# A hybrid pooling / matrix-memory layer on one core: single first transfers, unread products, w_up's sums loaded in mid-step, and the last group's second norm moved into the feed-forward half

## The chip, the core and the metric

The kernel runs on one core of a Trainium2 chip. A core has a matrix engine (TensorE, PE in the profile; PEld are its weight loads), three engines for elementwise work (VectorE = DVE, ScalarE = ACT, GpSimd = POOL), and a queue engine (SyncE = SP) that does little but issue DMA transfers; ACT can issue transfers too. Each engine works through its own list of instructions in order and waits for the others on semaphores. On-chip memory is SBUF; products of PE land in eight PSUM banks.

The metric is the device time of one execution in microseconds (us). Matrix products have fp32 data, most of them split into two parts (`fp32r`, high and low) with three passes per product; a product of two plain fp32 operands shows as two records in the trace.

## The reference

One layer over 2112 tokens (2048 of a prompt and 64 of a sample with its own states), model width 1024, then a final norm. Cut to what matters:

```
mod = silu(c) @ w_ada + b_ada                 # shift, scale, gate: two times three vectors of 1024
h   = rmsnorm(x, g1) * (1 + sc1) + sh1
proj = h @ w_in                               # 512 pooling columns, q, k, v, o of 4 heads x 128, gates
pool_out = causal moving means of widths 2, 4, 8, 16, then a 128 x 128 product per group
hs  = mLSTM(q, k, v, gates)                   # chunked matrix memory, per-head norm, times sigmoid(o)
x   = x + gt1 * (concat(pool_out, hs) @ w_out)
h2  = rmsnorm(x, g2) * (1 + sc2) + sh2
up  = h2 @ w_up                               # 1024 -> 2 x 2816
conv = causal depthwise convolution of width 3 over tokens
x   = x + gt2 * ((silu(g) * a) @ w_down)      # 2816 -> 1024
y   = rmsnorm(x, g_final)
```

Also returned are the pooling, memory and convolution states at the end.

## The kernel before

Activations are held transposed, features on the 128 partitions and tokens along the free axis, so a row of 1024 features is eight tiles (`KD = 8`).

**Attention half.** Four groups of tokens: three of 512 and a last one of 576 (512 of the prompt and the 64 of the sample). Per group: the first norm, the projections, the memory and the pooling mixer, the output projection `outproj` with the residual, whose result goes to DRAM as `x2d`. A scheduler orders the instructions of this half by priorities and costs of its own, so an edit in one place can move instructions elsewhere; only the first part of group 0, `first()`, is in the order as written (`tc.manual_schedule`).

`first()` begins with no data on the chip. The first 512 tokens of x come as eight tiles `x0[k]`, then V (a table with small vectors, and the 128 x 128 identity), then the four loads of the first quarter of the modulation weights (`w_mod`). ACT squares each x0 tile (L984), DVE adds the squares into two sums (L989), `rstd_cols` (L485) adds over partitions with one-column products (L489) and makes the reciprocal root (DVE L491, then POOL). `mod_q` (L918) makes a quarter of the modulation vectors: 32 products of a two-column operand (L923), a copy by ACT (L930), a transpose on PE (L932). Four products (L1001) spread the norm's factors over partitions into the bank `pr`; DVE multiplies x by it (L1005); ACT shifts and scales (L953), and the first projection (L1028) can start. Products whose result nobody reads stand in between (L991 on each x0 tile, and L1010).

**Background work.** Lists `bg[0]` to `bg[4]` hold generators; `tick(i)` advances one of them by one step between pieces of the main work. In groups 1 to 3 these run: `ada` (the remaining modulation vectors from `w_ada`: loads `raw<-w_ada` and multiply-adds on DVE, L197), `fold`, and `up_sums` (L819). The latter works ahead for the feed-forward half: for each of 44 pieces of w_up it loads four parts (`w<-w_up`, two transfers, L824), takes sums and differences in four DVE operations (L838, L839, L841, L842) and stores the piece (`wsum<-w`, L847). The order of these instructions among themselves is kept; where they stand among others is the scheduler's choice. There are four buffers for the pieces. `gemm` (L435) is the product loop, with line L445 for its products. In the middle of each group `lstm` copies gate values out of PSUM: CL (after which a cumulative product L1201 follows), GL (which products at L1255 free their bank by), then kw (read by the products L1280).

**Last group's second norm.** `outproj` ends with the squares of the new x for the second norm: an ACT square (L476, L479) and a DVE add (L480) per row, in `sq_acc`. For the last group the sum then goes to `stat2` (L578), which waits twelve ticks in the feed-forward half and calls `rstd_cols`.

**Feed-forward half.** All in the order as written. Three groups of 704 tokens, in four parts of the 22 blocks of 128 inner features. Seven products per block instead of eight come from sums and differences of inputs and weights (`norm_sums` L771 makes those of the inputs, hx: DVE L745 and others, ACT L738; `wsum` has those of the weights). `product` (L525, products L1531) works with weights that ACT and DVE split into two parts (L379, L382); ACT evacuates (s at L1570, u at L1579 and L1594), the convolution and gate follow, and the down projection is L1807 with its residual on DVE (L1823).

**The end.** The last part of the last group is done in two sections of tokens, 448 and 256 (`ENDS`). For each, `final_end` adds the squares over partitions (L1705), makes the factors (DVE L1661, POOL L1663), spreads them by products (`spread`, L1721), multiplies (DVE L1746, POOL L1759) and stores y. `m2_ps` and `mm_ps` hand out PSUM banks in rotation.

## Time and profile before

| | us |
|---|---|
| median of 3 runs (2225.89 to 2227.29) | 2227.15 |
| the profiled execution | 2230.81 |
| its span from first to last instruction | 2229.0 |
| PE busy | 2208.9 |
| DVE busy | 1572.2 |
| ACT busy | 1000.4 |
| POOL busy | 192.5 |
| moved by DMA | 487.26 MB, 219 GB/s in the mean |

All times below that are called "at" are us from the start of the span. A row of a timeline gives start, duration (of the merged instructions), engine, line, operation, output <- inputs by the program's names, shapes and count; in brackets stands how long the engine had been idle and what ended that. The clock of PE is given in the windows as a share of its full speed. A row of the chain of waits has start, duration and what it was.

### The profile page before, as it was taken

How to read it: one execution, taken by the hardware profiler on the slowest of the kernel's cores; microseconds unless marked ns; L12 is line 12 of the kernel's file. 1: busy time of each engine (PE TensorE's matmuls, PEld its weight loads, DVE VectorE, ACT ScalarE, POOL GpSimd, SP SyncE). 2: the span in 40 equal slices, each digit the busy share in tenths (PEclk: the TensorE clock that was granted, in tenths of full speed). 3: DMA queues.
4: the chain of work that ended last, by engine and by line, in shares of the span. 5: the costliest groups of instructions: out<-in, count | busy, mean ns of one | idle time of the engine just before them, and what ended most of it. 6: DMA issues, size and time to landing. Idle time of an engine off the chain costs nothing.

```text
span 2229.0 us, 37990 instructions
## 1 busy us (share of the span) xinstructions
PE 2208.9 (99%) x13744; PEld 2102.7 (94%) x13744; DVE 1572.2 (71%) x2888; ACT 1000.4 (45%) x1981; POOL 192.5 (9%) x474
## 2 busy tenths in 40 slices
PE   8999999999999999999999999999999999999998
PEld 7888888888899999999999999999999999999998
DVE  5867668757955688687858587777766675757475
ACT  4644335234333455454536354545444343445254
POOL 0010000001000100010000210100001210101012
PEclk9999999999999999999999999999999999999999
DMA  9977997988879485747557775466458655353442
GB/s 350 330 251 228 300 305 254 306 286 266 296 253 299 148 269 164 243 163 270 179 176 243 263 263 176 156 213 198 143 160 290 196 167 167 111 171 116 145 148 81
DMA packets 284708, 487.26 MB, mean 219 GB/s; under 512 B 24640, under 2 KB 88512, under 8 KB 284520
## 3 DMA queue, kind: packets, MB, share of 16 engines
q1 hardware_dynamic: 275080, 462.52, 63.2%
q10 hardware_dynamic: 9440, 22.32, 2.6%
q8 instruction: 108, 1.77, 0.3%
q14 instruction: 80, 0.66, 0.1%
HBM read 378.68 MB, written 106.06 MB: 217 GB/s over the span
## 4 chain that ended last, share of the span: by engine, by line
PE 94%; DMA 3%; DVE 2%; issue 1%; SPq 0%; ACT 0%; POOL 0%; POOLq 0%; DVEq 0%; ACTq 0%
PE mm L1531 40%; PE mm L1807 23%; PE mm L445 23%; PE mm L1091 1%; DMA raw<-w_ada 1%; PE m L1280 1%; PE m L1300 1%; PE m L1302 1%; PE m L1265 1%; DMA wsum<-w 1%; PE mm L1028 1%; PE p L1028 1%; PE m L923 0%; PE m L1255 0%; DVE scr L237 0%
## 5 line engine op out<-in xcount | busy, mean ns | idle before, releaser
L1531 PE MATMUL mm<-hx,wt 128*128 128x352 f32 x5544 | 897.9, 323 | 1.9 <-ACT s L1570 1.3
L1531 PEld LDWEIGHTS mm<-hx,wt 128*128 128x128 f32 x5544 | 892.8, 188 | 2.6 <-ACT s L1570 1.6
L1807 PE MATMUL mm<-av,wt 128*128 128x352 f32 (+2 forms) x3168 | 514.5, 323 | 0.0
L1807 PEld LDWEIGHTS mm<-av,wt 128*128 128x128 f32 x3168 | 509.6, 188 | 1.2
L445 PE MATMUL mm<-hl,wt 128*128 128x512 f32 (+2 forms) x1920 | 389.7, 358 | 0.0
L379 ACT ACTIVATE wt<-raw 128x512 fp32r<-128x512 f32 (+3 forms) x518 | 286.2, 574 | 215.6 <-PE mm L445 77.6
L382 DVE TENSOR_TENSOR wt<-raw,wt 128x512 fp32r<-128x512 f32 (+3 forms) x518 | 324.4, 641 | 78.4 <-ACT wt L379 75.6
L445 PEld LDWEIGHTS mm<-hl,wt 128*128 128x128 f32 x1920 | 315.4, 189 | 52.5 <-issue 5.3
L1823 DVE SCALAR_TENSOR_TENSOR x<-mm,MOD,x 128x352 f32<-128x352 f32 (+4 forms) x224 | 106.5, 526 | 133.1 <-PE mm L1807 132.9
L445 PE MATMUL mm<-mx,wt 128*128 128x512 f32 (+1 forms) x960 | 185.3, 354 | 0.0
L445 PEld LDWEIGHTS mm<-mx,wt 128*128 128x128 f32 x960 | 159.1, 188 | 25.4
L1518 DVE SCALAR_TENSOR_TENSOR tg<-eg,V,tg 128x704 f32<-128x704 f32 (+1 forms) x132 | 125.7, 953 | 53.9 <-ACT tg L1513 51.6
L382 DVE TENSOR_TENSOR wt<-wt 128x512 fp32r<-128x512 f32 x176 | 121.7, 692 | 36.9 <-ACT wt L379 36.9
L1518 DVE SCALAR_TENSOR_TENSOR ta<-ea,V,ta 128x704 f32<-128x704 f32 (+1 forms) x132 | 125.7, 952 | 5.2 <-ACT ta L1513 2.6
L379 ACT ACTIVATE wt<-wt 128x512 fp32r<-128x512 f32 x176 | 108.3, 622 | 18.3 <-DMA wt<-wsum 14.6
L1579 ACT ACTIVATE u<-mm 128x352 f32<-128x352 f32 x66 | 30.7, 465 | 169.5 <-PE mm L1531 162.0
L1539 DVE TENSOR_TENSOR eg<-mm,u 128x352 f32<-128x352 f32 x154 | 70.2, 468 | 41.2 <-ACT u L1594 27.1
L1639 DVE TENSOR_TENSOR av<-tg,av 128x704 fp32r<-128x704 f32 (+1 forms) x88 | 60.6, 709 | 53.8 <-ACT av L1634 53.8
L1625 ACT ACTIVATE tg<-tg 128x704 f32<-128x704 f32 (+1 forms) x66 | 52.4, 794 | 78.5 <-DVE tg L1518 78.5
L1570 ACT ACTIVATE s<-mm 128x352 f32<-128x352 f32 x66 | 30.7, 465 | 111.4 <-PE mm L1531 106.9
L1091 PE MATMUL mm<-wt,hl 128*128 128x256 f32 (+1 forms) x576 | 70.7, 282 | 0.0
L1091 PEld LDWEIGHTS mm<-wt,hl 128*128 128x128 f32 x576 | 69.8, 188 | 0.9 <-issue 0.6
(293 smaller groups left out, 1954.3 us busy)
## 6 DMA issues: line engine op xcount, KB each, us to landing
raw<-w_up SPq DMA_DIRECT2D x198, 256.0 KB, 4.0
wt<-hl_kept SPq DMA_DIRECT2D x96, 512.0 KB, 6.0
wt<-wsum SPq DMA_DIRECT2D x176, 256.0 KB, 4.0
wt<-wsplit SPq DMA_DIRECT2D x88, 512.0 KB, 4.6
raw<-w_down SPq DMA_DIRECT2D x96, 256.0 KB, 3.0
w<-w_up SPq DMA_DIRECT2D x88, 256.0 KB, 4.0
wsum<-w SPq DMA_DIRECT2D x44, 512.0 KB, 5.1
wsplit<-wt SPq DMA_DIRECT2D x44, 512.0 KB, 3.3
```

What stands on the lines that cost most here:

```text
L379: act.activation(u.w[:, 0, :u.n], u.raw[:, :u.n], AF.Copy)
L382: dve.tensor_tensor(out=u.w[:, 1, :u.n], in0=u.raw[:, :u.n], in1=u.w[:, 0, :u.n].bitcast(F32), op=ALU.subtract)
L445: pe.matmul(ps[bi][:, :hi - lo], U[:, a, k % 4 * P:(k % 4 + 1) * P], mv[k][:, b, lo:hi], start=(at == 0 and pi == 0), stop=(k == order[-1] ...
L1028: pe.matmul(to[ti][:, :n], h[k][:, b, ti * P:(ti + 1) * P], w[:, a, k % 2 * n:(k % 2 + 1) * n], start=(hv == 1 and k == 0 and (a, b) == (0 ...
L1091: pe.matmul(ps[ti][:n, :cols], h[4 * kh + k4][:, b, lo:lo + n], U[:, a, k4 % 2 * cols:(k4 % 2 + 1) * cols], start=(kh == 0 and k4 == 0 and ...
L1518: dve.scalar_tensor_tensor(out=t[:, :E], in0=ext[:, j:j + E], scalar=wc(j, f), in1=t[:, :E], op0=ALU.mult, op1=ALU.add)
L1531: pe.matmul(ps[:, :FH], U[:, a, kc * P:(kc + 1) * P], Bo.at(nm, kc, b), start=(first and kc == 0 and pi == 0), stop=(kc == 3 and pi == 2), ...
L1539: dve.tensor_tensor(out=ext[:, d:d + b - a], in0=ps[:, a:b], in1=u[:, a:b], op=ALU.add)
L1625: act.activation(self.tg[:, :E], self.tg[:, :E], AF.Silu)
L1639: dve.tensor_tensor(out=self.d[:, 1, a:b], in0=self.tg[:, a + 2 * s:b + 2 * s], in1=self.d[:, 0, a:b].bitcast(F32), op=ALU.subtract)
L1807: pe.matmul(ps[i][:, :hi - lo], U[:, a, k % 4 * P:(k % 4 + 1) * P], av[k][:, b, lo:hi], start=(k == 0 and (a, b) == PASSES[0]), stop=(k == ...
L1823: dve.scalar_tensor_tensor(out=x3[n][:, a:b], in0=ps[i][:, a - lo:b - lo], scalar=gt2(n, s), in1=x3[n][:, a:b], op0=ALU.mult, op1=ALU.add)
```

## The change

- The eight tiles of x0 come in eight transfers of 256 KB, four each from SP and ACT, instead of four of 512 KB.
- In `first()`, squares 6 and 7 are not added by DVE; four sums go to PE, which adds them over partitions by accumulating one-column products into a bank that is cleared beforehand. The factors are spread by one product of `ones` with a diagonal matrix that DVE makes, instead of four products with the identity. Eight products that nobody reads stand between the eight steps of `mod_q(0)`, and the two at L1010 write to another bank.
- Two small operations on V (into M and GH) move from the front of DVE's list to behind `first()`.
- In `up_sums` a step i with 0 < i < len - 2 loads piece i + 2 ahead of its four DVE operations, where before it loaded piece i + 3 after them, ahead of the store.
- For the last group the squares and adds leave `outproj`. `stat2` reloads the eight rows from `x2d` and does squares, adds and `rstd_cols` in steps in the feed-forward half.
- In the last section of the end, the bank for the sums over partitions is taken and cleared before the last row's products, and products that nobody reads are put in two places (`busy`).

```diff
-    for k in range(0, KD, 2):
-        (act if k % 4 else nc.sync).dma_start(out=pair_of(x0[k:k + 2]), in_=xT[k:k + 2, :, 0:GT].rearrange("k p t -> p k t"))
+    for k in range(KD):
+        (act if k % 2 else nc.sync).dma_start(out=x0[k], in_=xT[k, :, 0:GT])
...
-    def stat2(o, ssum):
-        out = RS2[:, 4 * o.g:4 * o.g + len(o.chunks)]
-        for _ in range(12):
-            yield
-        rstd_cols([ssum], o, out)
+    def stat2(o):
+
+        def load(k):
+            x = fscr()
+            nc.sync.dma_start(out=x[:, :o.T], in_=x2d[k, :, o.t0:o.t0 + o.T])
+            return x
+        nx = [load(0), load(1)]
+        ssum = fscr("ssum")
+        yield
+        for k in range(KD):
+            x = nx.pop(0)
+            yield
+            act.activation((x if k else ssum)[:, :o.T], x[:, :o.T], AF.Square)
+            yield
+            if k:
+                dve.tensor_tensor(out=ssum[:, :o.T], in0=ssum[:, :o.T], in1=x[:, :o.T], op=ALU.add)
+            if k + 2 < KD:
+                nx.append(load(k + 2))
+        yield
+        rstd_cols([ssum], o, RS2[:, 4 * o.g:4 * o.g + len(o.chunks)])
         yield
...
-                if o.last:
-                    ssum = fscr("ssum")
             for n, x in zip(rows, xs):
-                sq_acc(ssum, x[:, :o.T], o.T, n == 0)
+                if not o.last:
+                    sq_acc(ssum, x[:, :o.T], o.T, n == 0)
         if o.last:
-            bg[0].append(stat2(o, ssum))
+            bg[0].append(stat2(o))
...
                 yield
                 yield
+                if 0 < i < len(todo) - 2:
+                    nx.append(load(*todo[i + 2]))
...
                 yield
-
-                if i + 3 < len(todo):
-                    nx.append(load(*todo[i + 3]))
                 pin(nc.sync.dma_start(out=wsum[f, :, :, c:c + 256], in_=w))
...
+            cols = third.tile([P, 512], F32, tag="bank", name="cols")
+            dve.memset(cols[:, :4], 0.0)
             for k in range(KD):
                 x, sq = x0[k], scr()
                 act.activation(sq[:, :GT], x, AF.Square)
-                if k < 2:
+
+                if k < 2 or k > 5:
                     sums.append(sq)
...
             silu()
+            for sq in sums:
+                for ti in range(4):
+                    pe.matmul(cols[:, ti:ti + 1], sq[:, ti * P:(ti + 1) * P], ones[:, 0:1], start=False, stop=sq is sums[-1],
+                              skip_group_check=True)
             rs = sm.tile([P, 5], F32, tag="rs", name="rs")
-            rstd_cols(sums, o0, rs)
+            dve.tensor_scalar(out=rs[:, :4], in0=cols[:, :4], scalar1=1.0 / D, scalar2=EPS, op0=ALU.mult, op1=ALU.add)
+            pool.tensor_tensor(out=rs[:, :4], in0=rs[:, :4], in1=half[:, :4], op=ALU.pow)
             mod = mod_q(0)
-            for _ in range(KD + 1):
+            for k in range(KD):
                 next(mod)
 
+                pe.matmul(ptq[:, 256:384], x0[7][:, :P], x0[7][:, :P], start=True, stop=True)
+            next(mod)
+            dg = scr()
+            dve.tensor_tensor(out=dg[:, :GT].rearrange("p (t c) -> p t c", c=P),
+                              in0=ident.unsqueeze(1).broadcast_to([P, 4, P]),
+                              in1=rs[:, 0:4].unsqueeze(2).broadcast_to([P, 4, P]), op=ALU.mult)
             pr = third.tile([P, 512], F32, tag="bank", name="pr")
-            for ti in range(4):
-                pe.matmul(pr[:, ti * P:(ti + 1) * P], rs[:, ti:ti + 1].broadcast_to([P, P]), ident, start=True, stop=True)
+            pe.matmul(pr, ones, dg[:, :GT], start=True, stop=True)
...
             for _ in range(2):
-                pe.matmul(psq[:, :256], x0[7][:, :P], x0[7][:, :256], start=True, stop=True)
+                pe.matmul(ptq[:, 256:], x0[7][:, :P], x0[7][:, :256], start=True, stop=True)
...
                     ps_v = first()
+                    dve.tensor_copy(M[:, GT + 1:GT + 2], RV[:, 2:3])
+                    dve.tensor_scalar(out=GH, in0=V[:, V_GH:V_GH + NH], scalar1=0.5, scalar2=None, op0=ALU.mult)
...
-    late, YLATE = [], 6
+    late, early, YLATE = [], [], 6
+
+    def busy(n):
+
+        for _ in range(n):
+            pe.matmul(early[1][:, :P], ident, ident, start=True, stop=True)
...
-        ps = m2_ps()
+        ps = m2_ps() if lo == 0 else early[0]
...
-        if lo > 0:
-            dve.memset(ps[:, :len(tiles)], 0.0)
...
         if lo > 0:
             late[0](YLATE)
+            busy(3)
         stat_cols(ps, rs, [n for (t, n) in tiles])
...
                 if ends and n == KD - 1:
+                    if lo > 0:
+                        busy(2)
                     sq7 = fscr()
...
+                    if ends and n == KD - 1 and secs[0][0]:
+
+                        early.extend([m2_ps(), mm_ps()])
+                        dve.memset(early[0][:, :2], 0.0)
                     down(ps, rows[n], range(nf), secs, ends)
```

2 lines of the change are left out of this document (removed).

## The prediction

> **What bounds the kernel now.** I read the page first, then the list of PE's waits, then the windows around those waits. The first rows below are the page's busy times and the shares of its chain of waits; then the list of PE's waits (us in total, times, longest).
>
> ```profile
> PE 2208.9 (99%) x13744; PEld 2102.7 (94%) x13744; DVE 1572.2 (71%) x2888; ACT 1000.4 (45%) x1981; POOL 192.5 (9%) x474
> PE 94%; DMA 3%; DVE 2%; issue 1%; SPq 0%; ACT 0%; POOL 0%; POOLq 0%; DVEq 0%; ACTq 0%
> ```
>
> ```profile
> PE m L991 <- DMA mx<-xT: 5.7, 1, 5.7
> PE m L1255 <- DVE GL L237: 2.0, 1, 2.0
> PE m L1280 <- DVE kw L237: 2.0, 1, 2.0
> PE mm L1531 <- ACT s L1570: 1.3, 1, 1.3
> PE m L489 <- DVE scr L989: 1.0, 2, 0.9
> PE m L1721 <- POOL rs L1663: 1.0, 1, 1.0
> PE m L1705 <- DVE m L1702: 0.9, 1, 0.9
> PE mm L1028 <- ACT hl L953: 0.6, 1, 0.6
> PE mm L1531 <- DVE hx L745: 0.6, 1, 0.6
> ```
>
> TensorE (PE) is busy 99% and is 94% of the chain. So no edit to another engine counts unless it ends one of these nine waits (15.1 us together), or shortens a stretch in which PE is busy with less than products. Three places hold nearly all: the start (5.7 + 1.0 + 0.6), the middle of each attention group (2.0 + 2.0) and the seam to the feed-forward half with the end (1.3 + 0.6 + 1.0 + 0.9). Beside that PE loses time to its granted clock; the windows are cut where it changes (columns: busy time of each engine, clock, DMA share, GB/s).
>
> ```profile
> 10.64:14.06 3.42, 2.38 (x16) 1.84 (x14) 2.53 (x5) 1.50 (x4) 0.00 (x0) 1.00 1.05 387
> 14.06:17.47 3.41, 3.41 (x47) 2.80 (x50) 0.16 (x1) 0.00 (x0) 1.10 (x2) 0.50 1.05 390
> 17.47:20.88 3.41, 3.41 (x40) 2.65 (x33) 0.00 (x0) 0.81 (x2) 0.00 (x0) 0.50 1.06 387
> 20.88:24.29 3.41, 2.79 (x16) 2.02 (x16) 2.98 (x9) 2.25 (x5) 0.00 (x0) 1.00 1.05 396
> 263.23:266.64 3.41, 1.45 (x10) 1.00 (x9) 2.51 (x5) 0.19 (x1) 0.00 (x0) 1.00 0.80 267
> 266.64:270.06 3.42, 3.42 (x13) 3.00 (x13) 3.03 (x9) 0.00 (x0) 0.00 (x0) 0.50 1.04 335
> 2219.05:2222.46 3.41, 1.51 (x12) 1.29 (x11) 2.94 (x8) 1.02 (x3) 0.81 (x2) 1.00 0.68 259
> ```
>
> The clock halves for a whole window of 3.41 us after a window that was poor in work: 1.45 of 3.41 busy, 1.51 busy (what comes after it is in the last rows of this text, 1.79 against 1.19 us for eight like records), but also 2.38 busy, mainly with one-column products. The window from 14.06 was fully busy with one- and two-column products and did not bring it back; the next, half of it 128-column products (L1001), did. So thin products hardly count, by this trace.
> The Trainium skill (TensorE: Matmul & The Clock Gate, "What's actually happening") says that the gate watches a free-running window of 3413 ns and halves the clock after an idle window; the length agrees with the 3.41 us here, the condition does not, since none of these windows was idle.
>
> The sum goes against the profiled execution, 2230.81 us (span 2229.0). That is 3.7 us over the median of the runs, 2227.15; I subtract the sum from the median.
>
> **A, the start** (single transfers; no wait for V; sums 6 and 7 added by PE; L1001 as one product; unread products between).
>
> ```profile
> 5.67 6.16 PE L991 MATMUL m<-mx 128*128 128x256 f32 x16 [5.67 <-DMA mx<-xT]
> 15.58 3.59 PE L923 MATMUL m<-mx,CA 128*2 128x128 f32 x64
> 19.10 1.99 PE L1001 MATMUL pr<-V,rs 128*128 128x128 f32 x8
> 20.93 0.27 PE L932 MATMUL m<-V,scr 128*128 128x128 f32 x1
> 21.04 1.03 PE L1010 MATMUL m<-mx 128*128 128x256 f32 x4
> 22.69 2.04 PE L1028 MATMUL mm<-wt,hl 128*128 128x264 f32 x11 [0.62 <-ACT hl L953]
> 33.00 1.86 PE m L923 x64
> 9.35 0.14 DVE L1420 COPY M<-V 4x1 f32<-4x1 f32 x1 [7.95 <-DMA V<-vecs]
> 820.14 0.99 PE m L489 x10
> ```
>
> Before, the products on x begin at 5.67 with the landing of a 512 KB pair, and take 6.16 us without a gap. DVE's adds wait 7.95 us behind a copy from V, so the sums on PE end only where L923 begins, at 15.58. After: half the pair is 256 KB, and with two queues in flight 0.5 MB less stands before the first landing; at the 390 GB/s of the windows that is 1.3 us, so PE starts at about 4.4 and is through at 10.5. The Trainium skill (DMA: Bandwidth & Descriptors, "Bandwidth") speaks against this edit: transfers below 1 MiB get less of the peak, 341 GB/s at 1 MB and 138 at 64 KB; an estimate of 250 GB/s at 256 KB by it would land the 2 MB of x about 3 us later. The window from 20.88, where 264 KB and 256 KB loads stand in the queue, moved 396 GB/s, so I add nothing for it.
>
> The copies from V leave the queue ahead of the adds, four adds remain instead of six, and V's later issue (its queue slot now waits for a landing) holds up only SiLU and the ident product, both needed after 12 us. On PE there are now 32 one-column passes instead of 16. At full clock one costs 0.99/10 = 0.10 us, so 3.2 us: 10.5 to 13.7, against 15.58 before. Then come 64 records of the modulation, 1.86 us at full clock (the row at 33.00) or 3.59 at half, and between them 16 records of unread 128-column products, 0.15 each at full (1.19/8, the row at 2213.61 below) or 0.22 at half (1.79/8): 4.3 us at full, 7.1 at half. One 512-column product replaces L1001: as many columns as the four L1010 records, 1.0 us at full clock against 1.99. From the small transpose (L932) to the first projection (L1028) it stays 22.69 - 20.93 = 1.76 us.
> At full clock throughout: 13.7 + 4.3 + 1.0 + 1.8 = 20.8. If x's products run partly at full clock (they begin earlier, so an earlier window may already count) all of it comes some 0.7 sooner: 20.1. If the clock is half from 13.7 until 17.5, when a window with the unread products has passed, 3.8 of the 7.1 us are done, the rest takes 2.0, and it is 22.3; with a window more at half clock about 23.2. Gain: 2.6 at best, -0.5 at worst. I take 1.9, the value at full clock, because the window from 17.47 shows that such a mixture raises it. The loads are no obstacle: the DMA share is full in these windows with the same bytes, and PE's next loads have slack because PE had waited for none of them (no such row among the waits).
>
> **D, the sums of w_up in mid-step.** Loads two ahead are issued ahead of the four DVE operations, not three ahead after them; 44 steps in groups 1 to 3. No work is added. What moves is SP's order: a load now waits for its buffer's store (a store of sums needs 5.1 us to land) ahead of w_ada's loads, and other things end up behind it.
>
> ```profile
> wsum<-w SPq DMA_DIRECT2D x44, 512.0 KB, 5.1
> 640.82 0.42 DVE L838 TENSOR_TENSOR w<-w 128x256 f32<-128x256 f32 x1 [6.68 <-DMA w<-w_up]
> 448.34 0.69 DVE L237 TENSOR_TENSOR kw<-m,CL 128x512 f32<-128x512 f32 x1 [3.06 <-PE m L1255]
> 449.67 1.05 PE L1280 MATMUL m<-va,kw 128*128 128x129 f32 x8
> ```
>
> In group 1 the wait of 2.0 at L1280 is on kw, which stands behind an operation on a w_ada load; in the new order that load follows no fewer stores of sums, so this stays. In group 3 the wait of 2.0 at L1255 is there because the copy GL stands in DVE's queue behind a step whose load landed at 640.8. In the new order GL comes free sooner, but an earlier step stands ahead of the copy CL, so up to 2.0 may come back at L1201. In group 2 nothing waits now; kw ends at 449.03, 0.64 ahead of its product, and it moves behind a later load. Bounds: -2.0 and +2.0; I take -0.5. If the cover in group 2 goes, it costs up to 2 us and a half-clock window.
>
> **E, the second norm of the last group.**
>
> ```profile
> 808.54 1.07 DVE L237 SCALAR_TENSOR_TENSOR scr<-mm,MOD,scr 128x256 f32<-128x256 f32 x3
> 810.82 0.76 DVE L480 TENSOR_TENSOR ssum<-ssum,scr 128x576 f32<-128x576 f32 x1
> 821.17 0.22 DVE L491 TENSOR_SCALAR RS<-m 128x4 f32<-128x4 f32 x2 [4.44 <-PE m L489]
> 809.69 0.69 ACT L479 ACTIVATE scr<-scr 128x576 f32<-128x576 f32 x1 [0.96 <-DVE scr L237]
> 821.06 24.26 PE L1531 MATMUL mm<-hx,wt 128*128 128x352 f32 x149
> ```
>
> Eight squares (0.69) and seven adds (0.76) leave the last output projection. The waits of 0.6 and 1.3 at L1531 are on DVE's hx and on ACT's s, which stand behind these: three of the adds (2.3 us) from 800 on, and, after the late row evacuation at 808.54, a square at 809.69 ahead of s. In the new order DVE has the hx operations done ahead of the last evacuation; both waits go, 1.9 us. The work returns under the first pair: 5.5 us on ACT, 5.3 on DVE (now idle there for 4.4 us at one stretch alone), plus eight reloads on SP (2.4 MB, 6 us at 390 GB/s, put ahead of weight loads of the same stretch); the cover is the 24 us of products from 821.06. Late next is L489: PE meets it 36 records later, and the last add needs the last square, which follows s, two splits, a square and ta on ACT. From the product that s reads these are seven operations with the add; at the 0.69 of the square's row 4.8 us (an estimate), while PE gets there in 30 products of 24.26/149 = 0.163: 4.9. So a wait of 0 to 0.5; I take 0.2. E: -1.7 (bounds -1.9 and +0.5, if reloads delay splits).
>
> **F, the end.**
>
> ```profile
> 2213.61 1.19 PE L1721 MATMUL m<-V,rs 128*128 128x128 f32 x8
> 2219.77 0.51 ACT L1833 ACTIVATE fscr<-x 128x192 f32<-128x192 f32 x2 [0.95 <-DVE x L1823]
> 2220.52 0.58 PE L1705 MATMUL m<-ones_r,fscr 128*128 128x1 f32 x4
> 2222.14 1.79 PE L1721 MATMUL m<-V,rs 128*128 128x128 f32 x8 [1.04 <-POOL rs L1663]
> ```
>
> The memset wait of 0.9 on PE is not worth 0.9: the last products need the square that ACT ends at 2220.28, and they start at 2220.52 now. So 0.2. Two unread products (0.6) fill the gap before, three (0.9) the POOL wait of 1.0. If the clock holds, the spread takes 1.19 instead of 1.79, and the rows behind it come 0.6 sooner. Bounds -1.0 and +0.3 (unread products at half clock outlast the wait). I take -0.8.
>
> Sum: -1.9 - 0.5 - 1.7 - 0.8 = -4.9; against the profiled execution 2225.9, against the median 2227.15 - 4.9 = 2222.3.
>
> **Rivals.** (1) The clock does not answer to the unread products: windows with 1.45 busy dropped, and 1.5 is what F puts in. Then the start gives 0.4 (22.3), the end 0.2: 0.4 + 0.5 + 1.7 + 0.2 = 2.8, 2224.3. Speaking against it is the window from 17.47. By the skill's rule named above the unread products would change nothing, since no gap at the end reaches a window; the two halved windows contradict the rule. (2) The work of E is late at L489, 1.5 us, and takes most of its gain: 2223.6 (1.3 above the forecast, 0.2 being in it). For it speaks that the path to its last square is as long as the products before it. (3) All covers hold: start 2.6, the 2.0 in group 3, 1.9, 1.0, together 7.5: 2219.7. For it: all four bounds are in rows above; against it: they must meet. (4) The other side: D's load, waiting a whole landing (5.1 us) ahead of w_ada's loads, delays kw in all three groups. Less the 0.6 of slack in group 2 that is 3 x 5.1 - 0.6 = 14.7; less the other gains (4.4) it is +10.3: 2237.4. It turns the sign when it delays each group by 1.5. Against it: the store ahead is a step old when the load comes.
>
> **How the numbers follow.** 0.2% is 4.45 us, about what a measurement can tell from no change. Chances: forecast 0.44 (own range 2220.5 to 2223.7; 0.34 of the 0.44 below 2222.7), rival 1 0.22, rival 2 0.10, rival 3 0.15, rival 4 0.09. Faster 0.34 + 0.15 + 0.04 of rival 1 and 2 at their lower ends = 0.53; slower 0.09; the same 0.38. The range 2218.0 to 2226.5 holds rivals 1 to 3 with their bounds and leaves rival 4 and some tails out.
>
> **What would show it.** First projection at 20 to 21.5 instead of 22.69, and full clock from about 14 on; no DVE wait for V ahead of the adds. Waits at L1531's successor gone, and none at the moved L489 above 0.3. No wait at L1280 in group 2; GL's wait in group 3 gone, and whether one at L1201 stands for it. At the end no row of half clock after 2219, and the spread in 1.2 us. The prediction is wrong if a wait of more than 2 us appears in a group's middle, or the first projection stays past 22.

## The result

The changed kernel takes 2240.68 us (median; 2239.52 to 2244.68) against 2227.22 (2225.89 to 2228.59) before, measured side by side: a ratio of 1.0063, 95% interval 1.005 to 1.0076. It is slower, by 13.5 us, where 2222.3 was forecast. The profiled execution took 2241.01, its span is 2239.2, 10.2 longer than the span before; what follows explains these 10.2. The other 3.3 lie in the choice of executions: the profiled one of before took 2230.81, 3.6 over its median, that of the changed kernel 0.3 over its own.

First the page's row of busy times of the changed kernel, then its list of PE's waits. (Lines from L596 on have moved: L1531 is now L1557, L1280 L1306, L1255 L1281, L991 L1007, L923 L936, L1001 L1027, L1010 L1036.)

```profile
PE 2216.5 (99%) x13780; PEld 2107.3 (94%) x13780; DVE 1570.1 (70%) x2888; ACT 1000.8 (45%) x1981; POOL 193.8 (9%) x474
```

```profile
PE m L1007 <- DMA mx<-xT: 4.5, 1, 4.5
PE m L1306 <- DVE kw L237: 3.9, 2, 2.2
PE mm L1557 <- DVE eg L1565: 3.0, 1, 3.0
PE m L1117 <- DVE scr L237: 2.0, 1, 2.0
PE m L1291 <- ACT at L237: 1.7, 1, 1.7
PE mm L1557 <- DVE ea L1609: 0.8, 1, 0.8
PE m L1036 <- DVE MOD L949: 0.5, 1, 0.5
PE m L1161 <- ACT va L237: 0.3, 1, 0.3
PE m L1751 <- POOL rs L1689: 0.3, 1, 0.3
PE m L1734 <- ACT fscr L1865: 0.2, 1, 0.2
```

The old waits did go: ACT's s and DVE's hx at the feed-forward seam (1.3 and 0.6), GL (2.0), the memset at the end (0.9), most of the POOL wait (1.0 to 0.3), and 1.2 of the first landing. But these rows add up to 17.2 (4.5 + 3.9 + 3.0 + 2.0 + 1.7 + 0.8 + 0.5, and 0.8 for the last three) against 15.1 before: a second kw, eg, scr and at have come. And PE is busy 7.6 us longer: it has 36 more records (26 of unread products and 16 of thin one-column passes more, 6 of the spread fewer), and the new ones at the start are on its path.

Where the 10.2 us come from is seen by laying equal products of the two traces beside each other (start after less start before):

| place | after less before, us |
|---|---|
| first product on x (4.51, was 5.67) | -1.2 |
| small transpose (23.57, was 20.93) and first projection (25.33, was 22.69) | +2.6 |
| at 56, group 0 | +3.1 |
| group 2, products L1306 (453.37, was 449.67) | +3.7 |
| group 3, L500, ahead of the late L1117 (611.75, was 607.97) | +3.8 |
| group 3, L1281, ahead of GL's place (647.73, was 640.17) | +7.6 |
| group 3, after GL's place (648.19, was 642.83) | +5.4 |
| first product of the feed-forward half (812.55, was 805.02) | +7.5 |
| after its seam (885.04, was 874.35) | +10.7 |
| end of the span | +10.2 |

So the start costs 3.1, the groups 7.5 - 3.1 = 4.4, the seam 3.2, and the end gives back 0.5. A row can hold more than a wait. From 3.8 to 7.6 in group 3 are 2.0 of waiting at L1117 and then a window of 3.41 at half clock (from 616.7), which takes 1.7. Before has such a window behind its kw wait in group 1 (from 266.64); the changed kernel has the same wait there (2.21 at 269.84) and keeps the clock. Which wait is followed by half clock differs between traces, so a single row is good to about 1.7.

**The start.** PE's rows and the windows by clock of the changed kernel:

```profile
4.51 5.96 PE L1007 MATMUL m<-mx 128*128 128x256 f32 x16 [4.51 <-DMA mx<-xT]
10.31 4.83 PE L1011 MATMUL cols<-ones_r,scr 128*128 128x1 f32 x32
15.06 0.61 PE L936 MATMUL m<-mx,CA 128*2 128x128 f32 x8
...
19.81 0.40 PE L936 MATMUL m<-mx,CA 128*2 128x128 f32 x8
20.14 0.49 PE L1020 MATMUL m<-mx 128*128 128x128 f32 x2
20.56 0.40 PE L936 MATMUL m<-mx,CA 128*2 128x128 f32 x8
...
22.71 1.02 PE L1027 MATMUL pr<-scr,ones_r 128*128 128x512 f32 x2
```

```profile
9.08:12.50 3.42, 3.42 (x28) 3.27 (x26) 0.13 (x1) 0.79 (x3) 0.00 (x0) 1.00 1.03 390
12.50:15.91 3.41, 3.41 (x22) 2.96 (x23) 0.16 (x1) 0.00 (x0) 0.49 (x1) 0.50 1.05 393
15.91:19.32 3.41, 3.41 (x30) 1.52 (x29) 0.69 (x1) 0.00 (x0) 0.61 (x2) 0.50 1.06 387
19.32:22.74 3.42, 3.42 (x47) 1.97 (x44) 0.00 (x0) 0.21 (x2) 0.00 (x0) 1.00 1.05 389
```

PE begins early and never stops, and is late all the same. The 32 thin passes take 4.83, not 3.2. The modulation with the unread products runs from 15.06 to 22.71, 7.65 us, where it took 3.59 before; nothing but PE's own work holds it up, as the next product on PE follows at once throughout. Two windows are at half clock, as many as before (there from 14.06); they begin after a window in which PE was busy throughout. The clock is not the whole of it: at full clock, in the window from 19.32, one of the eight steps (eight thin records, two unread ones) takes 0.75 us, from 19.81 to 20.56, so all eight would take 6.0.

**Group 2.** The timeline around the second kw wait, of the changed kernel:

```profile
441.75 1.25 SPq L838 DMA_DIRECT2D w<-w_up  x2
443.70 1.31 SPq L181 DMA_DIRECT2D raw<-w_ada  x2
450.21 0.75 DVE L197 SCALAR_TENSOR_TENSOR s<-raw,CA,s 128x512 f32<-128x512 f32 x1 [3.10 <-DMA raw<-w_ada]
452.54 0.68 DVE L237 TENSOR_TENSOR kw<-m,CL 128x512 f32<-128x512 f32 x1
453.37 1.13 PE L1306 MATMUL m<-va,kw 128*128 128x129 f32 x8 [1.70 <-DVE kw L237]
```

The next row is from the kernel before: there the last load of w_ada ahead of kw had left SP 5.3 us earlier, ahead of a pair of w_up.

```profile
438.38 0.95 SPq L181 DMA_DIRECT2D raw<-w_ada  x1
```

Now SP issues w_up's piece first and w_ada's loads after it. DVE waits 3.10 for the first of them, until 450.21, and kw stands behind that operation in DVE's list. Group 3 has the same picture at another place: w_up's pair at 605.71, w_ada's load at 607.06; DVE waits 3.35 for it, then makes the value that PE waits 2.03 for.

```profile
614.17 0.75 DVE L197 SCALAR_TENSOR_TENSOR s<-raw,CA,s 128x512 f32<-128x512 f32 x1 [3.35 <-DMA raw<-w_ada]
615.82 2.15 PE L1117 MATMUL m<-wt,hl 128*64 128x256 f32 x12 [2.03 <-DVE scr L237]
```

**The seam.** SP's issues, then the engines' rows around PE's longest new wait, of the changed kernel:

```profile
813.04 3.48 SPq L582 DMA_DIRECT2D fscr<-x2d  x4
817.06 0.32 SPq L623 DMA_DIRECT2D x2d<-scr  x1
817.47 0.38 SPq L582 DMA_DIRECT2D fscr<-x2d  x1
823.11 0.87 SPq L1678 DMA_DIRECT2D x<-x2d  x2
824.08 0.86 SPq L366 DMA_DIRECT2D wt<-wsum  x2
```

```profile
829.59 0.63 ACT L379 ACTIVATE wt<-wt 128x512 fp32r<-128x512 f32 x1 [3.76 <-DMA wt<-wsum]
830.12 0.67 ACT L590 ACTIVATE fscr<-fscr 128x576 f32<-128x576 f32 x1
...
830.82 0.76 DVE L593 TENSOR_TENSOR ssum<-ssum,fscr 128x576 f32<-128x576 f32 x1 [5.30 <-ACT fscr L590]
831.50 0.52 DVE L1565 TENSOR_TENSOR eg<-mm,u 128x352 f32<-128x352 f32 x1
832.16 1.22 PE L1557 MATMUL mm<-hx,wt 128*128 128x352 f32 x3 [2.96 <-DVE eg L1565]
```

Seven of the eight reloads leave before 818, six of them ahead of the store of a row of x2d at 817.06. A load of residual rows then stands at the head of SP's queue until 823.11, and SP's list of waits says for what: for that store's landing. The first row below is from the changed kernel, the second from before.

```profile
SPq L1678 <- DMA x2d<-scr: 5.2, 1, 5.2
SPq L1652 <- DMA x2d<-scr: 1.8, 1, 1.8
```

Before, the store left at 809.63 and the load could follow at 811.85, 2.2 us later; behind the reloads this takes 6.0. The weights behind that load leave at 824.08, 11.5 after the first product of this half (812.75 before, 7.7 after it), and land at 829.56. ACT's split waits 3.76 for them, the square behind it is late, DVE's add waits 5.30 for the square, eg stands behind the add, and PE waits 2.96 for eg. PE's window from 831.70 to 835.11 is then at half clock. Both engines had stood still for most of the time; of E's own work one square and one add lie between the landing and eg, some 1.3 us. Of the 3.2 of the seam 1.9 are waits (3.8 against 1.9), the rest is the half-clock window.

**The end.** The spread (L1751) is not slowed any more, and of the waits 0.3 and 0.2 are left. From the end of the last down product to the end of the span it is 9.29 instead of 9.80.

### The profile page after: what moved, and what is told of

Read it like the earlier page. It is cut to its first block, busy times and chain, and to the rows that moved or that the text cites. A ratio compares the mean times of both kernels' runs of the same rounds, so it can differ in the third digit from the quotient of the medians.

```text
span 2239.2 us, 38084 instructions
## 1 busy us (share of the span) xinstructions
PE 2216.5 (99%) x13780; PEld 2107.3 (94%) x13780; DVE 1570.1 (70%) x2888; ACT 1000.8 (45%) x1981; POOL 193.8 (9%) x474
## 3 DMA queue, kind: packets, MB, share of 16 engines
q8 instruction: 109, 1.79, 0.3%
## 4 chain that ended last, share of the span: by engine, by line
PE 94%; DMA 3%; DVE 1%; issue 1%; ACT 0%; SPq 0%; POOL 0%; POOLq 0%; DVEq 0%; ACTq 0%
PE mm L1557 39%; PE mm L445 23%; PE mm L1837 23%; PE mm L1117 2%; DMA raw<-w_ada 1%; PE m L1306 1%; PE m L1328 1%; PE m L1326 1%; PE m L1291 1%; DMA wt<-wsum 1%; PE m L936 0%; PE mm L1054 0%; PE m L1281 0%; PE m L873 0%; PE m L1007 0%
## 5 line engine op out<-in xcount | busy, mean ns | idle before, releaser
L1557 PE MATMUL mm<-hx,wt 128*128 128x352 f32 x5544 | 899.1, 323 | 3.8 <-DVE eg L1565 3.0
L1557 PEld LDWEIGHTS mm<-hx,wt 128*128 128x128 f32 x5544 | 894.1, 188 | 4.4 <-ACT wt L379 4.3
L445 PE MATMUL mm<-hl,wt 128*128 128x512 f32 (+2 forms) x1920 | 388.8, 358 | 0.0
L445 PEld LDWEIGHTS mm<-hl,wt 128*128 128x128 f32 x1920 | 314.7, 188 | 52.4 <-issue 5.3
L445 PE MATMUL mm<-mx,wt 128*128 128x512 f32 (+1 forms) x960 | 185.3, 354 | 0.0
L445 PEld LDWEIGHTS mm<-mx,wt 128*128 128x128 f32 x960 | 159.1, 188 | 25.4
L1117 PE MATMUL mm<-wt,hl 128*128 128x256 f32 (+1 forms) x576 | 71.8, 285 | 0.0
L1117 PEld LDWEIGHTS mm<-wt,hl 128*128 128x128 f32 x576 | 70.9, 191 | 0.9 <-issue 0.6
```

The lines of the kernel that those rows point to most:

```text
L445: pe.matmul(ps[bi][:, :hi - lo], U[:, a, k % 4 * P:(k % 4 + 1) * P], mv[k][:, b, lo:hi], start=(at == 0 and pi == 0), stop=(k == order[-1] ...
L1117: pe.matmul(ps[ti][:n, :cols], h[4 * kh + k4][:, b, lo:lo + n], U[:, a, k4 % 2 * cols:(k4 % 2 + 1) * cols], start=(kh == 0 and k4 == 0 and ...
L1557: pe.matmul(ps[:, :FH], U[:, a, kc * P:(kc + 1) * P], Bo.at(nm, kc, b), start=(first and kc == 0 and pi == 0), stop=(kc == 3 and pi == 2), ...
```

## The experiments

**Each part alone.** Four kernels carry one part of the change each. e_start has all edits of the first part:

```diff
+    for k in range(KD):
+        (act if k % 2 else nc.sync).dma_start(out=x0[k], in_=xT[k, :, 0:GT])
...
+                if k < 2 or k > 5:
...
+                pe.matmul(ptq[:, 256:384], x0[7][:, :P], x0[7][:, :P], start=True, stop=True)
...
+            pe.matmul(pr, ones, dg[:, :GT], start=True, stop=True)
```

e_sums has the loads of up_sums alone:

```diff
+                if 0 < i < len(todo) - 2:
+                    nx.append(load(*todo[i + 2]))
...
-                if i + 3 < len(todo):
-                    nx.append(load(*todo[i + 3]))
```

e_norm2 has the second norm alone:

```diff
+            act.activation((x if k else ssum)[:, :o.T], x[:, :o.T], AF.Square)
...
+                nx.append(load(k + 2))
...
-                sq_acc(ssum, x[:, :o.T], o.T, n == 0)
+                if not o.last:
+                    sq_acc(ssum, x[:, :o.T], o.T, n == 0)
```

e_end has the end alone:

```diff
+            busy(3)
...
+                        busy(2)
...
+                        early.extend([m2_ps(), mm_ps()])
+                        dve.memset(early[0][:, :2], 0.0)
```

> The kernel before with the edits of the start alone (single transfers, four sums on PE, one product for the spread, unread products). Theory, from the changed kernel's trace (offset of equal products against before): the start alone costs 2.6 us at the first projection and 3.1 by 60 us, because the unread products stand on PE's own path at half clock; nothing later is touched, so about 2230.0. Rival: the later waits in the groups' middles are set off by the later start, so this edit alone brings most of the 13 us: 2235 or more. My prediction's own step A would give 2225.3.

> The kernel before with the sums of w_up loaded in mid-step alone. Theory: the new order on SP and DVE makes the waits by itself, 1.7 at L1280 in group 2 and 2 to 3.5 in group 3, while the wait at GL (2.0) goes: between 4 and 5 us slower, about 2231.5. Rival: the waits were due to the later start; alone this edit is within 1 us of before.

> The kernel before with the second norm of the last group in the feed-forward half alone. Theory: the eight reloads and the row loads of x stand on SP ahead of the weight loads of the first pairs, so a wait of about 3 us appears at L1531 near 820, with a half-clock window behind it, against 1.9 us of waits saved: about 3 us slower, 2230.5. Rival (my step E): the waits were made by other lateness; alone the edit gains 1.7, 2225.5.

> The kernel before with the edits of the end alone (bank cleared early, five unread products). Theory, from the changed kernel's trace: the end is 0.5 us shorter, 2226.7; the clock still halves at the end. Rival (my step F): with the clock held 0.8 shorter, 2226.4; the trace must show whether the spread runs at full clock.

| part alone | time, us | ratio to before, 95% interval |
|---|---|---|
| before, same chip | 2229.2 | |
| start | 2233.18 | 1.0014 (1.0003 to 1.0025) |
| sums | 2236.87 | 1.0036 (1.0024 to 1.0048) |
| second norm | 2229.9 | 1.0000 (0.9991 to 1.001) |
| end | 2228.14 | 0.9996 (0.9986 to 1.0005) |

Together 0.14 + 0.36 + 0.00 - 0.04 = 0.46%, against 0.63 (0.50 to 0.76) for the whole change. The sums are the largest part, the start the second. No part is a clear gain. In e_sums kw is late in groups 1 (2.23 at 266.64, as before) and 2 (2.18 at 452.30, new), GL's wait is gone, but further on in group 3 CL is waited for (0.79 at 640), and at 698 and 705 PE waits for ACT (2.58, 1.41):

```profile
PE m L1279 <- DVE kw L237: 4.4, 2, 2.2
PE mm L445 <- ACT k L1208: 2.6, 1, 2.6
```

These waits are 9.2 us against 4.0 in the same groups before, which is most of the 5.9 by which this trace's span is longer. The one at 705 comes from another load: DVE waits 3.46 for `mx<-x2d` until 702.29, ACT's work on mx follows, and at stands behind it in ACT's list. What SP waited for between 225 and 800 changed too (the first two rows are before, the others e_sums):

```profile
SPq L824 <- DMA wsum<-w: 100.4, 36, 5.8
SPq L847 <- DVE w L842: 18.2, 16, 3.1
SPq L824 <- DMA wsum<-w: 51.7, 23, 5.8
SPq L846 <- DVE w L844: 36.0, 19, 5.7
```

A load of w_up stands less at the head of the queue for its buffer's store to land, 51.7 us instead of 100.4; the store stands there longer for its sums, 36.0 instead of 18.2, with the other loads behind it. That this second wait makes them late no run tests by itself.

In e_norm2 both old waits at the seam go, as forecast, with 0.5 left at L489, and an eg wait comes; the offset goes from -0.9 at the first product of the feed-forward half to -0.4 at 874, so the seam alone costs 0.5 where 1.7 was to be gained (no half-clock window follows here):

```profile
821.61 3.12 PE L1545 MATMUL mm<-hx,wt 128*128 128x352 f32 x18 [1.87 <-DVE eg L1553]
825.26 1.26 PE L489 MATMUL m<-ones_r,ssum 128*128 128x1 f32 x10 [0.53 <-DVE ssum L593]
```

**The start without its eight unread products.** The diff is against e_start.

```diff
-                pe.matmul(ptq[:, 256:384], x0[7][:, :P], x0[7][:, :P], start=True, stop=True)
```

> The edits of the start alone, without the eight unread products between the steps of the modulation. Theory: with the unread products the modulation took 7.65 us on PE (15.06 to 22.71 in the changed kernel) against 3.6 without them at half clock, and PE, not a landing, was the bound there; without them the first projection comes 3.5 to 4 us sooner than in the start alone, at 21 to 22, and the run is 2 to 4 us shorter than that one, at or below before. Rival: the clock matters more, and without the unread products it stays at half longer, so that little is won: within 1 us of the start alone.

2230.07 against 2228.26: 1.0004 (0.9995 to 1.0013). The first projection starts at 20.91, though the clock was at half from 14.64 to 24.88; with the unread products it starts at 25.33 in the changed kernel and at 26.82 in e_start, 4.4 and 5.9 later. So in the traces the unread products are the start's whole loss: they stand on PE's own path. The times (1.0014 and 1.0004) point the same way, but their intervals overlap. Did the unread products raise the clock? In e_start, with all of them, it stayed at half from 15.75 to 29.41, through four windows, in three of which PE never stopped:

```profile
12.34:15.75 3.41, 3.41 (x44) 2.48 (x43) 0.60 (x2) 0.00 (x0) 1.10 (x2) 1.00 1.05 394
15.75:19.17 3.42, 3.42 (x32) 1.82 (x30) 0.26 (x1) 0.00 (x0) 0.00 (x0) 0.50 1.05 386
19.17:22.58 3.41, 3.41 (x30) 1.74 (x23) 0.00 (x0) 0.38 (x2) 0.00 (x0) 0.50 1.05 389
22.58:25.99 3.41, 2.89 (x7) 1.24 (x6) 1.13 (x6) 0.81 (x2) 0.00 (x0) 0.50 1.05 408
25.99:29.41 3.42, 3.42 (x15) 3.15 (x14) 3.35 (x6) 2.96 (x6) 0.00 (x0) 0.50 0.92 329
```

**Only the transfers and the adds that don't wait for V.** Of the start, the eight transfers and the two moved operations on V are kept; sums, factors and products are as before.

```diff
+    for k in range(KD):
+        (act if k % 2 else nc.sync).dma_start(out=x0[k], in_=xT[k, :, 0:GT])
...
+                    dve.tensor_copy(M[:, GT + 1:GT + 2], RV[:, 2:3])
+                    dve.tensor_scalar(out=GH, in0=V[:, V_GH:V_GH + NH], scalar1=0.5, scalar2=None, op0=ALU.mult)
```

> Of the edits of the start only the single transfers and the two small operations on V behind first(); six adds, sixteen one-column products and four products for the spread as before, no more unread products than before. Theory (a part of step A was right: the adds no longer wait for V, DVE has both sums by about 10.5, and PE needs only 16 passes): the sums on PE end near 12.5 and the last load of the modulation (14.7 to 14.9) becomes the bound; the modulation is through at 15.5 to 17, first projection 19 to 21. Against before, which in five profiles had it at 19.8 to 22.8, that is 1 to 2 us: 0.05 to 0.1% faster. Rival (the clock rules): with the thinner work the clock is at half longer and the gain goes, 0 or slower.

In its trace the first projection is at 18.86 instead of 22.69, the clock never lost; best1 and best2 (below), with the same start, have it at 18.36 and 18.48. w_mod's landings are late next (0.39 and 0.74), and further on PE waits for ACT:

```profile
53.12 0.27 PE L1134 MATMUL m<-V,gt 128*4 128x128 f32 x1 [1.48 <-ACT va L237]
```

So a part of the lead is lost again by 53. The product behind this block (L445) starts at 53.76 to 54.64 in the three traces with this start and at 54.45 to 56.17 in the ten with the old one: 1.4 us earlier in the mean, with ranges that overlap a little. The measured time is 2229.43 against 2227.84: 1.0004 (0.9995 to 1.0013), no gain; 1.4 us would lie just outside that interval. The profile's span is 5.3 us shorter than before (2223.7), but it is of this kernel's shortest execution (2225.49, median 2229.43), and that of before is of one above its median; so the median of all executions decides.

**Depth or place of the sums' loads.** d_depth2 (first diff) loads two ahead, not three, at the old place; d_mid3 (second) three ahead at the new place.

```diff
-                if i + 3 < len(todo):
-                    nx.append(load(*todo[i + 3]))
+                if 0 < i < len(todo) - 2:
+                    nx.append(load(*todo[i + 2]))
```

```diff
+                if i + 3 < len(todo):
+                    nx.append(load(*todo[i + 3]))
...
-                if i + 3 < len(todo):
-                    nx.append(load(*todo[i + 3]))
```

> The sums of w_up with loads two ahead instead of three, but issued at the old place, after the four operations. Theory: the harm is that the two transfers of the next piece stand ahead of w_ada's and x2d's loads (place), so this costs less than half of the 6 to 8 us of the edit: within 3 us of before. Rival: the depth is what changes the order; then as slow as the whole edit.

> The sums of w_up with loads three ahead as before, but issued in mid-step, ahead of the four operations. Here the load must wait for the store of the step just before (same buffer), so the wait of a landing, 5 us, stands in SP's queue. Theory (place): at least as slow as the whole edit, 6 us or more over before, with kw waiting in group 2. Rival (depth): within 2 us of before.

d_depth2: 1.0017 (1.0008 to 1.0026). d_mid3: 1.0048 (1.0034 to 1.0062). Both cost. The place costs 0.48% with three ahead; with two it is 0.36 against 0.17, whose intervals just overlap. In d_mid3 every piece is asked for earlier than in the kernel before, and DVE's waits for pieces are hardly longer (10.1 us between 225 and 800, before 8.9), so little of its loss comes from pieces that are late themselves; what is left is what they are moved past. kw waits in groups 1 and 2 again (2.08 at 266.6, 2.40 at 452.8), and PE waits 1.8 for an operand's own load (`wt<-hl_kept`).

d_depth2, with the loads later than before, has other late ones (hx 3.0 at the seam, at 2.4, CL 1.5): each of the three shifts of these 44 loads that were run found instructions that had just enough room.

**The changed kernel with the old sums.**

```diff
-                if 0 < i < len(todo) - 2:
-                    nx.append(load(*todo[i + 2]))
...
+                if i + 3 < len(todo):
+                    nx.append(load(*todo[i + 3]))
```

> The changed kernel with the sums of w_up as before. Theory, adding the parts run alone: about 0.1% over before, so 5 to 9 us shorter than the changed kernel; the wait at eg at the seam to the feed-forward half, 3.0 there and 1.9 with the second norm alone, shows whether that wait grows with what stands before it. Rival: the parts act on each other, and less than 4 us of the 13 go.

2232.74 against 2228.26: 1.0017 (1.0006 to 1.0029). From 1.0063 to 1.0017 the sums are 0.46% of the changed kernel's 0.63, some 10 us, within the intervals what they cost alone. The kw waits are gone; the eg wait at the seam stays (2.27), with a half-clock window behind it, and the seam costs 1.7.

**w_ada asked for earlier.** If kw is late because w_ada's loads come late, a w_ada step at two places of each product row instead of one should bring them forward, with the sums in mid-step as changed. The step also comes ahead of that of up_sums now. The diff is against e_sums.

```diff
+            if at in (1, 4) and not quiet and not spare:
+                tick(3)
...
-            if at == 4 and not quiet and not spare:
-                tick(3)
```

> The sums of w_up in mid-step, with a step of w_ada's work at two places of each product row instead of one, so that w_ada's loads and multiply-adds are through sooner in each group. Theory (w_up's loads stand ahead of w_ada's, and the gate's path and kw behind w_ada's operations on DVE): the waits at kw in groups 1 and 2 go, 3 us or more shorter than the edit, within 4 us of before. Rival (any new order of this half costs as much): as slow as the edit, 6 to 8 us over before, with waits at other places.

2234.41 against 2228.18: 1.0026 (1.0016 to 1.0035), below the 1.0036 of e_sums, though the intervals overlap. Group 2's kw wait falls from 2.18 to 0.39, as the chain from w_ada's load to kw asks. But the time comes back as waits on other loads in the same stretch (1.16 and 0.85 for `wt<-hl_kept` at 445.04 and 449.16), and group 1's kw still waits 2.0.

**The second norm's reloads.** e_norm2_act issues the reloads from ACT instead of SP, and begins 16 ticks later. e_norm2_noload leaves them out: the squares are of one constant column, so the work on ACT, DVE and PE is as in e_norm2 and only the transfers are missing. Both diffs are against e_norm2.

```diff
-            nc.sync.dma_start(out=x[:, :o.T], in_=x2d[k, :, o.t0:o.t0 + o.T])
+            act.dma_start(out=x[:, :o.T], in_=x2d[k, :, o.t0:o.t0 + o.T])
...
+        for _ in range(16):
+            yield
```

```diff
-            act.activation((x if k else ssum)[:, :o.T], x[:, :o.T], AF.Square)
+            act.activation((x if k else ssum)[:, :o.T], V[:, 0:1].broadcast_to([P, o.T]), AF.Square)
```

> The second norm of the last group in the feed-forward half, with its reloads issued from ACT's queue and sixteen ticks later, so that they do not stand on SP ahead of the row loads and weight loads of the first pairs. Theory (SP's order and the transfers ahead made the wait at eg): the wait of 1.9 to 3.0 at eg goes, the two old waits (0.6 and 1.3) stay away, and the run is 1 to 2 us faster than before. Rival (the work itself, squares and adds among the splits, makes the wait): a wait of 2 us or more at L1531's products near 820 remains.

> The second norm of the last group in the feed-forward half, but without its eight reloads: the squares are taken of a constant column instead of the rows (so the factors of the last group's second norm are left wrong and the transfers left out; squares, adds and products are as many as in the edit). Theory (the transfers make the wait): no wait above 0.5 at the seam, and 1 to 2 us faster than before. Rival (the engine work among the splits): a wait of 1.5 to 2 at eg as with the reloads, and the same time as before.

From ACT, and 16 ticks later: 1.0035 (1.0023 to 1.0048), worse; which of the two edits did it no run tells apart. PE runs through the seam without a gap until 829, then waits 1.6, 2.6 and 1.9; ACT's squares wait for their reloads (1.92, 0.36, 1.37 and 1.32 in the rows of one stretch), and the splits of the weights stand behind the squares. Without reloads: 2226.71 against 2228.18, 0.9994 (0.9984 to 1.0003), and the seam has one wait left, the 0.5 at L489, that the forecast had as its bound:

```profile
819.97 1.26 PE L489 MATMUL m<-ones_r,ssum 128*128 128x1 f32 x10 [0.51 <-DVE ssum L591]
```

Its offset falls from -4.25 at the first product of the feed-forward half to -5.68 at 874, a gain of 1.4 at the seam; the time alone, whose interval reaches 1, would not show it. Against e_norm2, which lost 0.5 there, the transfers cost 1.4 + 0.5 = 1.9 us by these two traces, and this turns E from a gain into nothing. The chain is the one at the seam above: SP waits 1.8 for the store of x2d without the reloads, 4.6 with them.

**The end without unread products.** The diff is against e_end.

```diff
-            busy(3)
...
-                    if lo > 0:
-                        busy(2)
```

> The bank of the end cleared early, without the five unread products. Theory: 0.2 to 0.3 of the 0.5 us remain (the first products over the sums start sooner), and the clock halves in the window before the spread, which takes 1.8 instead of 1.2. Rival: the whole gain is the early bank's and the clock's fall depends on its window alone.

0.9992 (0.9982 to 1.0001), like e_end's 0.9996. From the last down product to the end of the span it is 9.24, with the unread products 9.26, before 9.80. In this kernel the spread runs 1.45 at a falling clock behind a wait of 1.04, in the changed one in 1.16 behind 0.27 (at 2232.56), and the end comes no earlier:

```profile
2218.77 1.45 PE L1724 MATMUL m<-V,rs 128*128 128x128 f32 x8 [1.04 <-POOL rs L1663]
```

So the half microsecond is the early bank's, and the unread products earn nothing. Nor do they show that they hold the clock: the spread takes 1.16 in all five traces that have them, but also in eight of the twelve that don't (before, with 1.79, is one of the other four).

**Combinations.** best1 is a_light with e_end, best2 that with e_norm2_act.

> The kernel before with the light start and the edits of the end. If the gains add: 1 to 2 at the start and 0.5 to 0.9 at the end, 0.1% faster. If the start's gain is only a matter of the clock's phase: within 0.05% of before.

> The light start, the edits of the end and the second norm with reloads from ACT; w_up's sums as before. If the gains add: 3 to 4 us, 0.15% faster than before and about 0.8% faster than the changed kernel. If the second norm's work makes its own wait: as the kernel without it.

1.0006 (0.9997 to 1.0015) and 1.0036 (1.0023 to 1.0049). No combination that was run beats the kernel before.

## Why the prediction was wrong, by its steps

**D, the sums: the step "I take -0.5" between bounds of -2 and +2.** It is the largest miss: 0.36% alone, about 8 us, and 0.46%, about 10 us, within the change. Of the two sentences about kw, that for group 2 came true ("it moves behind a later load ... up to 2 us": 1.7 to 2.2), and that for group 1 had it right that its wait stays. The failure was twofold: the gain of GL, which did come, was weighed against this as if they were equal, and only these few instructions were looked at. The runs put in their place late w_ada loads ahead of kw in group 2 and of L1117 in group 3, and in e_sums a late load of x2d ahead of at. Rival 4 (a load ahead of w_ada's loads delays kw) had this side, at 0.09, and its 2237.4 is the nearest of all; but that is in part luck. Its reason, a whole landing waited for ahead of w_ada's loads in all three groups, did not come: SP's wait for these landings fell from 100.4 us to 51.7, and kw has a new wait in group 2 alone. In the rows w_ada's loads come behind w_up's in SP's order: in group 2 w_up's pair left at 441.75, w_ada's at 443.70, and DVE waited 3.10. d_ada_more agrees with the chain from load to kw, and shows that bringing those loads forward makes others late. Of the 7.7 us of e_sums its trace shows 5.9; its profiled execution is at its median (2236.81, 2236.87) and that of before 1.6 over the median on this chip, which is the rest.

**A, the start: the step "I take 1.9, the value at full clock".** The start lost 2.6 to 3.1 in the trace (0.14% alone, also about 3 us), outside its bounds of -2.6 to +0.5. The term that failed is the 4.3 us for the modulation with the unread products between. It took 7.65, and this is not the clock alone: at full clock a step takes 0.75 and all eight 6.0; at half clock a step takes 1.27 (15.06 to 16.33), all eight 10.2, where 7.1 was put. The prices came from rows of like products in one run (64 thin ones in 1.86, eight of 128 columns in 1.19); mixed as here, they cost more, why is open. With 6.0 in place of 4.3 the sum at full clock gives 22.5 for the first projection, and next to nothing is gained on the 22.69 of before. The 3.2 for the 32 thin passes became 4.83, as they ran partly in a half-clock window; in the three other traces that have them, at full clock, they took 3.63. The reason given for full clock, that the window from 17.47 "shows that such a mixture raises it", was an inference from one window, and e_start contradicts it. Rival 1 was right here that the clock does not answer, but not in its price: its 22.3 still had the clock back at 17.5, and the projection came at 25.33. Without the unread products it came at 20.91. The transfers were right: first products at 4.51 for 4.4, and no loss by the smaller size. The estimate from the Trainium skill (DMA: Bandwidth & Descriptors, "Bandwidth") that was weighed there did not come true: the filled queue, with loads of 256 to 512 KB, moved 390 GB/s in the window from 9.08.

**E, the second norm: the step that named the cover, "24 us of products from 821.06".** Both waits at L1531 went, and L489 waited 0.5, at the bound of the term: these hold. What failed is that the eight reloads were priced as bytes (2.4 MB, 6 us at 390 GB/s) beside free time. They stand ahead of a store of x2d, a row load behind it waits for that store's landing at the head of SP's queue, and the weights that the splits need stand behind this load: 4.6 us of waiting in e_norm2 and 5.2 in the changed kernel, 1.8 without reloads. The bound "+0.5, if reloads delay splits" had the mechanism; e_norm2 hits it. In the changed kernel the seam costs 3.2, with a longer eg wait and a half-clock window behind it that e_norm2's trace does not have. e_norm2_noload's trace has nearly the forecast's gain (1.4 for 1.7) once the transfers are away.

**F, the end: right in sign, 0.5 for 0.8.** The term "0.6 us sooner if the clock holds" is void: the clock held and nothing came sooner.

**The sum.** The parts were forecast at -4.9; alone they measured about +3, +8, 0 and -1, together +10. The whole change cost 13.5. The 3 us between them lie inside what four intervals of about 0.1% each, and that of the whole, leave open. The forecast also took its gains of clock from one execution, 3.7 us over the median, and subtracted them from the median: the two half-clock windows of its start and the 1.79 of its last spread are not in most executions that were profiled, so of these gains a part at best could be had there.

## What to carry to other kernels

When a kernel's loads run through one queue, an edit that moves one load forward is priced by what it is moved past: list the loads and stores behind it, and for each the instruction that stands behind its landing on the engine that uses it. Products put in to keep a clock up stand on the path themselves when PE never waits there, so their cost is certain and their use is not; measure with and without them. Before a gain is read off one profile, compare that execution's time with the median: the profile of before was 3.6 us over it, that of a_light 3.9 below its own, and the 5.3 us between their spans were not in the measured times. A gain at the start should also be followed to the first waits behind it before it is booked.

## What the runs showed of the hardware

The granted clock was not what a share of busy time would tell. In e_start it was lost after a window that was busy throughout (from 12.34), and it stayed at half for four windows, three of them busy throughout; in the changed kernel it was lost after such a window too (from 9.08). In d_depth2, whose start is that of the kernel before, a window with 1.87 busy kept full clock and was followed by another at full:

```profile
10.16:13.57 3.41, 1.87 (x10) 1.31 (x8) 3.29 (x6) 1.94 (x4) 0.00 (x0) 1.00 1.05 387
13.57:16.99 3.42, 3.42 (x78) 3.14 (x78) 0.16 (x1) 0.00 (x0) 1.10 (x2) 1.00 1.05 388
```

In the kernel before, 2.38 busy in the window from 10.64 lost it. The grid of windows lies at another phase in each execution (it begins a window at 9.08, 10.16, 10.64 or 12.34 in these rows). Of ten traces with the same unchanged start, two lost no window on the way to the first projection and reached it at 19.76 (d_depth2) and 19.92, four lost one (21.11 to 21.27), and four, before among them, lost two (22.63 to 22.77): 1.4 us a window, and 3 us between the ends, more than the forecast's whole start term. The three traces with the light start lost none; those with all of the start's edits lost two (the changed kernel) or four (e_start, after_no_sums). The Trainium skill (TensorE: Matmul & The Clock Gate, "What's actually happening") has a busy window lift the throttle; in e_start the full windows from 15.75 and 19.17 did not, only that from 25.99 did, so for thin products with 128-column ones between them the measurement says otherwise. What the gate counts these runs do not settle: no threshold on busy time or on number of products fits all the windows seen.
